# Sums of weight blocks by adding transfers from DRAM to DRAM, for both MLP products of a decoder layer

## The chip, the core and the metric

The kernel runs on one core of a Trainium2 chip. The metric is the device time of one execution in microseconds (us). One execution was also recorded by the hardware profiler; all lines marked as profile come from that one. PE is TensorE (matmuls), DVE VectorE, ACT ScalarE, POOL GpSimd, SP the engine that issues most of the transfers. Each engine works through its own queue of instructions strictly in order.

## The reference

One decoder layer over 1024 positions of 1024 features, in float32. What matters here is its last part:

```python
for i in range(DEPTH):
    h = rms_norm(x, norm_mix[i])
    p = h @ w_in[i]
    ...                                   # RWKV-7 heads and a short convolution, gated and merged
    x = x + merged @ w_out_mix[i]
    mem_n = rms_norm(mem, norm_mem[i])
    x = x + memory_cross_attention(rms_norm(x, norm_xattn[i]), mem_n, w_q[i], w_kv[i], w_xo[i])
    hm = rms_norm(x, norm_mlp[i])
    x = x + jnp.square(jax.nn.relu(hm @ w_up[i])) @ w_down[i]
return rms_norm(x, norm_final)
```

`w_up` is 1024 x 4096 and `w_down` 4096 x 1024, 16 MB each.

## The kernel before

Activations are kept transposed, features on partitions and positions along the free side, in two blocks of 512 positions (b = 0, 1). Every float32 operand is split into a high and a low part (ACT rounds the high part, DVE subtracts to get the low part), and each product is three matmuls: high x high, high x low, low x high. Weights come as tiles of [128, 8, 128] (512 KB): a load into a raw buffer (`wr`, two of them; `wr+`, `wh+`, `wl+` and `P` are taken from the large pool `H`), then the split into `wh` and `wl`. `wlist` is the list of all weight tiles in the order of use, `w_loads` issues their loads on SP, `w_splits` the splits.

There is no fixed schedule: the program is written as many small streams, and a planner (`Scheduler`) that estimates every instruction's time runs whichever stream is ready and so writes each engine's order once, when the kernel is built. `need(t)` is the planner's time at which `t` is written, `done` holds the keys of steps that were issued, and `until(...)` waits for such keys. On the chip, only semaphores order the engines.

Both MLP products are done as two-by-two blocks with seven block products in place of eight (numbers 1, 2, 6, 5, 7, 3, 4). That needs sums of blocks of both operands. The products are the same count before and after the change: 16 steps of 7 products in `up_products`, and 7 products of 4 column tiles in `mlp_down`. The sums of the activations are made on DVE and POOL (`up_operands`, `sums`). For the weights, with blocks a11, a12, a21, a22, the before makes

- for `w_up`, inside the product: a "quad" of two raw tiles is loaded, POOL makes four sums in them (`w_split_quad`), and ACT and DVE split the pieces;
- for `w_down`, ahead of it: `w_sums` starts when the mixer's merge is done. In 16 rounds, SP loads four blocks, POOL makes four sums of 128 x 512, and SP stores them to `d_s`, from which the down product loads them as weight tiles.

The order of the kernel is: projections and RWKV (to about 735 us), keys and values of the 256 memory tokens (`mem_k`, `mem_v`, weights `w_kv`), merge (`w_proj_b`, `w_proj_a`), `w_out_mix`, queries and attention (`w_q`), its output product (`w_xo`, which adds the residual loaded from `d_x`), the up product, the down product, final norm. `norm_side` makes the reciprocal root mean square of a block of positions: a matmul with `ones` sums the squares (`pss<-ones,ex`), POOL takes the power.

Nearly every instruction has line L253, the planner's call, so rows are told apart by their tiles.

Of the kernel before, what the change touches and what calls it, by code (L numbers as in the profile page):

```python
# [9 lines left out]
F32 = mybir.dt.float32  # L10
F32R = mybir.dt.float32r
# [6 lines left out]
P = 128  # L18
# [240 lines left out]
def tile_hybrid_block(  # L259
# [116 lines left out]
    wlist, light, quads = [], set(), set()  # L376
# [11 lines left out]
    def w_quad(w, c0):  # L388

        return [(w[:, c0 + t * P:c0 + (t + 1) * P].rearrange("(k p) n -> p k n", p=P), 0, KD) for t in range(2)], \  # L390
            [P, KD, P]

    def w_block(half, t, j, kh):

        c0 = (2 * j + half) * P
        return w_down[0, kh * 2048:(kh + 1) * 2048, c0:c0 + P].rearrange("(k t p) n -> t p k n", t=2, p=P)[t]


    ws = {"raw": 0, "split": 0, "made": 0, "closed": 0, "next": 0, "live": 0, "raws": {}, "tiles": {}, "sums": 0}
    w_key = {}  # L400

    def w_raw(i):
        n = 2 if i in quads else 1
        more = i >= first_quad and (i - first_quad) % 2 if i in quads else i > first_quad and i % 4 > 1
        raw = ws["raws"][i] = [sb("wr+" if more else "wr", wlist[i][1]) for _ in range(n)]
        ws["live"] += n
        return raw

    def w_load(i, raw):
        for n, (src, k0, k1) in enumerate(wlist[i][0]):  # L410
            SP.dma_start(raw[n if i in quads else 0][:, k0:k1, :], src)
        ws["raw"] += 1

    def w_loads():
        for i in range(2, len(wlist)):
            if i < first_quad:
                yield lambda: i < ws["split"] + 2
            else:
                yield lambda: ws["live"] + (2 if i in quads else 1) + ws["sums"] <= BUFS["wr"] + 2
            if i in w_key:  # L420
                yield until(*w_key[i])
            raw = w_raw(i)
            yield need(*raw) - 0.3
            w_load(i, raw)

    def w_sums():

        yield until("merged")
        ws["sums"] = 2
        for j in range(4):  # L430
            for kq in range(4):
                kh, k0 = kq // 2, 4 * (kq % 2)
                t, keys = {}, []
                yield lambda: ("h2", 0, 5) not in done or ("h2r", 1) in done
                for pair in (((0, 0), (1, 0)), ((1, 1), (0, 1))):
                    raw = sb("wr+", [P, 2, 4, P])
                    for n, m in enumerate(pair):
                        yield need(raw)
                        t[m] = raw[:, n]
                        SP.dma_start(t[m], w_block(*m, j, kh)[:, k0:k0 + 4, :])  # L440
                a11, a21, a22, a12 = (t[m] for m in ((0, 0), (1, 0), (1, 1), (0, 1)))
                for n, (dst, x_, y_, op) in {7: (a11, a11, a21, ALU.subtract), 5: (a21, a21, a22, ALU.add),
                                             6: (a22, a22, a11, ALU.subtract), 3: (a12, a12, a22, ALU.subtract)}.items():
                    yield max(need(x_, y_), pace("POOL", 0.6))
                    POOL.tensor_tensor(dst, x_, y_, op=op)
                    keys.append(("s", n, j, kq))
                    dma(d_s[n][j, kh][:, k0 * P:(k0 + 4) * P], dst.rearrange("p k n -> p (k n)"), keys[-1])
                yield until(*keys)
        ws["sums"] = 0
# [5 lines left out]
    def w_split_quad(raws):  # L455


        n = KD // 2
        ra, rb = (t[:].rearrange("p (k t) n -> p t k n", t=2) for t in raws)

        def tiles():
            more = "+" if ws["made"] % 3 == 2 else ""
            return sb("wh" + more, [P, 2, n, P], F32R), sb("wl" + more, [P, 2, n, P], F32R)

        def halves(hi, lo, src):
            ACT.activation(hi, src, AF.Copy)
            yield need(hi) - 0.3
            DVE.tensor_tensor(lo, src, hi.bitcast(F32), op=ALU.subtract)

        room_ = lambda: ws["made"] < ws["closed"] + 3  # L470
        yield room_
        hi, lo = tiles()
        yield from halves(hi[:], lo[:], ra)
        w_made(hi, lo)
        yield need(lo)
        s2 = sb("st", [P, n, P])
        POOL.tensor_tensor(ra[:, 0], ra[:, 0], rb[:, 0], op=ALU.subtract)
        POOL.tensor_tensor(s2[:], rb[:, 1], ra[:, 0], op=ALU.subtract)
        POOL.tensor_tensor(rb[:, 0], rb[:, 0], rb[:, 1], op=ALU.add)
        POOL.tensor_tensor(ra[:, 1], ra[:, 1], s2[:], op=ALU.subtract)  # L480
        yield room_
        hi, lo = tiles()
        yield need(s2) - 0.3
        yield from halves(hi[:, 0], lo[:, 0], s2[:])
        yield need(rb) - 0.3
        yield from halves(hi[:, 1], lo[:, 1], rb[:, 0])
        w_made(hi, lo)
        yield room_
        hi, lo = tiles()
        yield need(ra) - 0.3  # L490
# [1602 lines left out]
```

## Time and profile before

| what | value |
|---|---|
| median of 3 runs | 1842.07 us (1840.36 to 1845.47) |
| profiled execution, its own time | 1842.19 us |
| its span, first to last instruction | 1840.5 us |
| mean granted TensorE clock | 0.977 |
| DMA | 289.19 MB, 157 GB/s mean |
| TENSOR_TENSOR `P<-P,P` on DVE | 204 of 770 ns |

Busy time is the time in which an engine works on an instruction; a matmul's includes its pipeline, so two that follow each other overlap. "idle before" and the words in brackets tell what ended the wait of an engine. In the chain of waits each piece is what the next one waited for, followed back from the end of the program. In rows by stretches the columns are PE, weight loads, DVE, ACT and POOL, then the granted clock, the busy share of the 16 DMA engines and what they moved. `SPq` rows are transfers that SP issues; their length is SP's time, not the transfer's.

### The profile page before, as it was taken

The page shows a single profiled execution, that of the slowest core. Times are in us where ns is not written, and L with a number is a line of the kernel's source. Part 1 is how long each engine was busy: PE and PEld are TensorE (multiplying, and loading weights), DVE is VectorE, ACT ScalarE, POOL GpSimd, SP SyncE. Part 2 cuts the span into 40 slices and gives each one's busy share as a digit, 9 for nine tenths or more (in the row PEclk, how much of TensorE's full clock was granted, in tenths as well). Part 3 has the DMA queues.
Part 4 walks back from the last instruction along what each step waited for, and adds up shares of the span by engine and source line. Part 5 has one row for each costly group of instructions (what it writes and reads, how often), then busy time and mean ns, then how long its engine had stood idle before and what let it go on. Part 6 is the DMA issues. An engine that isn't in the chain of part 4 may idle for free.

```text
span 1840.5 us, 26663 instructions
## 1 busy us (share of the span) xinstructions
PE 1773.6 (96%) x9914; PEld 1434.2 (78%) x9914; DVE 1078.3 (59%) x1689; ACT 698.8 (38%) x1229; POOL 514.6 (28%) x867
## 2 busy tenths in 40 slices
PE   7999999999989999999999999989999999999998
PEld 6577776767768778988888877868888888888887
DVE  4377665666564432456556765586777775655543
ACT  6423333123234332422233333354444444543442
POOL 2016653755536110000223445242323220000000
PEclk9699998999999999999999999999999999999999
DMA  6443532333325444754655667415454469765431
GB/s 211 168 125 104 157 112 61 104 82 104 105 66 169 119 126 126 228 167 149 229 180 166 206 192 263 126 60 190 145 183 144 163 203 336 266 211 198 165 113 60
DMA packets 302751, 289.19 MB, mean 157 GB/s; under 512 B 40648, under 2 KB 223038, under 8 KB 302622
## 3 DMA queue, kind: packets, MB, share of 16 engines
q1 hardware_dynamic: 302606, 287.49, 48.8%
q8 instruction: 78, 1.28, 0.3%
q14 instruction: 51, 0.42, 0.1%
q10 hardware_dynamic: 16, 0.00, 0.0%
HBM read 193.06 MB, written 94.37 MB: 156 GB/s over the span
## 4 chain that ended last, share of the span: by engine, by line
PE 67%; DVE 5%; DMA 3%; issue 2%; ACT 2%; POOL 1%; SPq 0%; POOLq 0%; DVEq 0%; ACTq 0%
PE psg L253 44%; PE pss L253 11%; PE psc L253 8%; PE psy L253 3%; DVE P L253 3%; DMA wr<-in_w_kv_dram 2%; ACT P L253 1%; DVE wl L253 1%; POOL ex L253 1%; ACT wh L253 0%; DMA P<-d_v 0%; DVE st L253 0%; DVE sh L253 0%; DVE sm L253 0%; DMA P<-d_x 0%
## 5 line engine op out<-in xcount | busy, mean ns | idle before, releaser
L253 PE MATMUL psg<-H,wh 128*128 128x512 f32 (+1 forms) x1872 | 614.3, 406 | 4.3 <-DVE P L253 3.7
L253 PEld LDWEIGHTS psg<-H,wh 128*128 128x128 f32 (+1 forms) x1872 | 353.5, 192 | 84.3 <-issue 4.0
L253 PE MATMUL psg<-P,wh 128*128 128x512 f32 (+1 forms) x1240 | 370.7, 380 | 3.3 <-ACT wh L253 1.8
L253 PE MATMUL psg<-H,wl 128*128 128x512 f32 x920 | 372.3, 405 | 0.4 <-DVE wl L253 0.4
L253 PEld LDWEIGHTS psg<-P,wh 128*128 128x128 f32 x1240 | 228.3, 189 | 47.2 <-ACT wh L253 2.4
L253 PE MATMUL psg<-P,wl 128*128 128x512 f32 (+1 forms) x620 | 235.4, 380 | 0.0
L253 ACT ACTIVATE wh<-wr 128x1024 fp32r<-128x1024 f32 (+2 forms) x189 | 139.5, 767 | 245.3 <-PE psg L253 134.1
L253 DVE TENSOR_TENSOR wl<-wr,wh 128x1024 fp32r<-128x1024 f32 (+2 forms) x180 | 166.0, 945 | 90.7 <-ACT wh L253 90.1
L253 PEld LDWEIGHTS psg<-H,wl 128*128 128x128 f32 x920 | 177.1, 193 | 37.6 <-DVE wl L253 1.0
L253 ACT ACTIVATE P<-P 128x512 fp32r<-128x512 f32 (+3 forms) x242 | 147.0, 641 | 73.2 <-DVE P L253 39.9
L253 DVE TENSOR_TENSOR P<-P,P 128x512 fp32r<-128x512 f32 (+2 forms) x204 | 149.6, 770 | 16.4 <-ACT P L253 15.0
L253 POOL TENSOR_TENSOR sm<-sm,mhalf 128x8 f32<-128x8 f32 (+2 forms) x18 | 23.8, 1327 | 440.9 <-DVE sm L253 440.9
L253 PEld LDWEIGHTS psg<-P,wl 128*128 128x128 f32 x620 | 116.8, 188 | 21.7 <-DVE wl L253 0.5
L253 POOL TENSOR_TENSOR ex<-ex,P 128x60 f32<-128x60 f32 (+24 forms) x248 | 94.1, 379 | 50.3 <-DMA P<-dn 34.0
L253 POOL TENSOR_TENSOR ex<-ex 128x60 f32<-128x60 f32 (+24 forms) x248 | 97.9, 395 | 19.4
L253 PE MATMUL pss<-P,wh 128*128 128x512 f32 x296 | 91.7, 390 | 1.2 <-DVE P L253 1.2
L253 DVE TENSOR_SCALAR P<-psc,sm 64x64 f32<-64x64 f32 x120 | 34.9, 291 | 85.2 <-ACT P L253 80.6
L253 PE MATMUL psc<-P,P 128*64 128x64 f32 (+4 forms) x816 | 75.0, 257 | 9.8 <-DVE P L253 4.9
L253 ACT ACTIVATE P<-psc,sm 64x64 f32<-64x64 f32 (+1 forms) x128 | 42.5, 333 | 105.5 <-PE psc L253 64.2
L253 PEld LDWEIGHTS psc<-P,P 128*64 128x64 f32 (+4 forms) x816 | 48.1, 147 | 44.1 <-issue 20.8
L253 DVE TENSOR_TENSOR P<-psg,P 128x512 f32<-128x512 f32 x44 | 30.3, 689 | 86.6 <-PE psg L253 69.4
L253 PE MATMUL psc<-P,wh 128*128 128x512 f32 x216 | 66.9, 390 | 0.0
(671 smaller groups left out, 2754.7 us busy)
## 6 DMA issues: line engine op xcount, KB each, us to landing
P<-d_t SPq DMA_DIRECT2D x56, 512.0 KB
wr<-in_w_in_dram SPq DMA_DIRECT2D x42, 512.0 KB
d_t<-P SPq DMA_DIRECT2D x64, 256.0 KB
d_x<-P SPq DMA_DIRECT2D x48, 256.0 KB
P<-d_x SPq DMA_DIRECT2D x24, 512.0 KB
d_t<-st SPq DMA_DIRECT2D x48, 256.0 KB
d_tg<-st SPq DMA_DIRECT2D x32, 256.0 KB
wr<-in_w_kv_dram SPq DMA_DIRECT2D x16, 512.0 KB
```

Source lines behind the costliest of these rows:

```text
L253: return fn(*args, **kw)
```

## The change

The sums of weight blocks are made from DRAM to DRAM, for both products. For each sum SP copies one block (`put`), and POOL's queue then issues a transfer that adds another block to the destination as it writes (`add`, `accum_op=ALU.add`). Since a transfer only adds, the seven products are rewritten with other signs: the second half of the output columns comes out negated (the operand of product 6 is split with its sign turned, relu takes the minimum instead of the maximum there and the square hides it, the down product's second half is subtracted). The column tiles that belong together are now half a weight apart (m = j + 4 * half) instead of neighbours.

```diff
-    def w_sums():
-        yield until("merged")
-        ws["sums"] = 2
-        ...                     # 16 rounds: four loads, four POOL tensor_tensor, four stores
-    def w_split_quad(raws):
-        ...                     # four POOL tensor_tensor for each quad of w_up, splits of the pieces
+    def w_half(w, t, half):
+        n = w.shape[1] // 2
+        rows = w.rearrange("(k t p) n -> t k p n", t=2, p=P) if w.shape[0] == D else \
+            w.rearrange("(t k p) n -> t k p n", t=2, p=P)
+        return rows[t][:, :, half * n:(half + 1) * n]
+    def w_sums():
+        yield until(("win", len(ORDER) - 1))
+        def put(dst, src):
+            yield from quiet()
+            yield need(dst, src)
+            SP.dma_start(dst, src)
+        def add(dst, src):
+            yield need(dst) + 1.0
+            POOL.dma_start(dst, src, accum_op=ALU.add)
+        for w, sums, key, n in ((w_up[0], d_su, "su", 1), (w_down[0], d_s, "s", 2)):
+            a11, a21, a12, a22 = (w_half(w, t, half) for t in range(2) for half in range(2))
+            for q in range(w.shape[0] // (2 * n * P)):
+                ks = slice(q * n, (q + 1) * n)
+                s5, s7, s6, s3 = (sums[p][ks] for p in (5, 7, 6, 3))
+                for dst, first, then in ((s5, a21, a22), (s7, a11, a21), (s6, s5, a11), (s3, s6, a12)):
+                    yield from put(dst, first if first in (s5, s6) else first[ks])
+                    yield from add(dst, then[ks])
+                yield need(s3)
+                done.add((key, q))
...
-    wlist += [w_quad(w_up[0], 2 * P * i) for i in range(NP_)]
+    d_su = {p: scratch([KD // 2, P, DFF // 2], f"d_su{p}") for p in (5, 7, 6, 3)}
+    for i in range(NP_):
+        cs = slice(i * P, (i + 1) * P)
+        for m, pair in enumerate((((0, 0), (1, 0)), (6, 5), (7, 3), ((1, 1),))):
+            srcs = [d_su[q] if q in d_su else w_half(w_up[0], *q) for q in pair]
+            if m in (1, 2):
+                w_key[len(wlist)] = [("su", q) for q in range(4)]
+            wlist.append(...)   # one tile: two loads of 256 KB (one for the last)
...
-        yield need(acc[b])
+        yield need(acc[b]) + (6.0 if key == "h3r" else 0.0)      # norm_side
...
-            DVE.scalar_tensor_tensor(dst, src, 0.0, r[b][:], op0=ALU.max, op1=ALU.mult)
+            DVE.scalar_tensor_tensor(dst, src, 0.0, r[b][:], op0=ALU.min if half else ALU.max, op1=ALU.mult)
...
-    nc = _bacc.Bacc("TRN2", target_bir_lowering=False, num_devices=1, dynamic_dma_scratch_size=256)
+    nc = _bacc.Bacc("TRN2", target_bir_lowering=False, num_devices=1, dynamic_dma_scratch_size=1024)
```

A round of `w_up` is 4 copies and 4 adding transfers of 1 MB (4 rounds), one of `w_down` the same of 512 KB (8 rounds). In each round two of the copies (`s6` from `s5`, `s3` from `s6`) read what an adding transfer has written, so SP waits for that transfer.

SP's queue in the keys and values of the memory. Before, loads of `w_kv` alternate with stores of the keys:

```order
L253 DMA wr_7010<-in_w_kv_dram 128x8x128
L253 DMA d_kt<-st_7016 128x256
L253 DMA wr_7056<-in_w_kv_dram 128x8x128
L253 DMA d_kt<-st_7050 128x256
L253 DMA wr_7086<-in_w_kv_dram 128x8x128
L253 DMA d_kt<-st_7096 128x256
L253 DMA wr_7130<-in_w_kv_dram 128x4x256
```

Now, at the same place (`d_su_84` and `d_su_85` are the sums 5 and 7 of `w_up`, 128x2048 is 1 MB):

```order
L253 DMA wr_7034<-in_w_kv_dram 128x8x128
L253 DMA d_kt<-st_7040 128x256
L253 DMA d_su_84<-in_w_up_dram 128x2048
L253 DMA d_kt<-st_7069 128x256
L253 DMA wr_7082<-in_w_kv_dram 128x8x128
L253 DMA wr_7108<-in_w_kv_dram 128x8x128
L253 DMA P_7128<-d_tg 128x1024
L253 DMA d_kt<-st_7121 128x256
L253 DMA wr_7164<-in_w_kv_dram 128x4x256
L253 DMA d_kt<-st_7159 128x256
L253 DMA wr_7191<-in_w_kv_dram 128x4x256
L253 DMA d_kt<-st_7204 128x256
```

The first copy of the fourth round now stands between the second and third of these loads, and the second (`d_su_85`) follows the rows shown.

SP's queue at the end of attention. Before, the residual's loads (`P<-d_x`) stand between the stores and loads of the w_down sums:

```order
L253 DMA wr+_1387_10123<-in_w_down_dram 128x4x128 x2
L253 DMA wr+_1395_10150<-in_w_down_dram 128x4x128 x2
L253 DMA d_s_87<-wr+_1387_10123 128x512
L253 DMA d_s_85<-wr+_1387_10123 128x512
L253 DMA P_10222<-d_x_133 128x1024
L253 DMA P_10224<-d_x_133 128x1024
L253 DMA d_s_86<-wr+_1395_10150 128x512
```

Now the last copy between sums, `d_s_91<-d_s_90`, stands here:

```order
L253 DMA d_s_91<-d_s_90 16x8192
L253 DMA st_9516<-d_vm 128x2x256
L253 DMA wr_9545<-in_w_xo_dram 128x8x128
L253 DMA wr_9709<-in_w_xo_dram 128x8x128
L253 DMA st_9767<-d_kt 128x2x256
L253 DMA st_9843<-d_vm 128x2x256
L253 DMA wr_9871<-in_w_xo_dram 128x8x128
L253 DMA wr_10031<-in_w_xo_dram 128x8x128
L253 DMA P_10129<-d_x_137 128x1024
L253 DMA P_10131<-d_x_137 128x1024
```

The sums have moved ahead of the loads of `w_xo`, and nothing of them is left around the residual's loads.

PE's queue at the end of `w_xo`'s product (`psg<-H`) and the start of the up product (`psg<-P`). Before, the sum of squares of the first block stands inside the former:

```order
L253 MATMUL psg_10854<-H_9952,wl_10724 128x512
L253 MATMUL pss_10879<-ones_128,ex_10247 128x1 x4
L253 MATMUL psg_10854<-H_10277,wh_10723 128x512
L253 MATMUL psg_10854<-H_10278,wh_10723 128x512
L253 MATMUL psg_10854<-H_10277,wl_10724 128x512
```

Now it comes within the second of the up product's sums:

```order
L253 MATMUL psc_10800<-P_10420,wl_10620 128x512
L253 MATMUL psc_10800<-P_10691,wh_10619 128x512 x2
L253 MATMUL pss_10812<-ones_132,ex_10149 128x1 x4
L253 MATMUL psc_10800<-P_10691,wl_10620 128x512
L253 MATMUL psc_10800<-P_10766,wh_10619 128x512 x2
```

It has moved behind the last matmuls with `H` and behind seven of the up product's eight first groups.

More of the change, by code (lines that the diff above doesn't have):

```diff
@@ L422, in w_loads @@
             raw = w_raw(i)
-            yield need(*raw) - 0.3
+            yield need(raw) - 0.3
             w_load(i, raw)
     def w_sums():
-        yield until("merged")
-        ws["sums"] = 2
[L430 to L449, printed above, removed]
+        yield until(("win", len(ORDER) - 1))
[16 more added lines that the diff above has]
+                done.add((key, q))
     def w_made(hi, lo):
@@ L453, in w_made @@
         ws["made"] += 1
-    def w_split_quad(raws):
[L458 to L490, printed above, removed]
-        yield from halves(hi[:], lo[:], ra)
-        w_made(hi, lo)
-        yield room_
-        hi, lo = tiles()
-        yield from halves(hi[:, 0], lo[:, 0], rb[:, 1])
-        w_made(hi, lo)
     def w_splits():
@@ L519, in w_splits @@
                 continue
-            more = "+" if i > first_quad and ws["made"] % 3 == 2 else ""
+            more = "+" if i > first_mlp and ws["made"] % 3 == 2 else ""
             hi = sb("wh" + more, wlist[i][1], F32R)
```

88 lines of the change are left out of this document (42 added, 46 removed).

## The prediction

> **What bounds the kernel now.** I read the page first (busy shares, slices, chain), then the busy time of each engine by stage, then the chain of waits and the timelines of single engines at the few places where TensorE stands still.
>
> ```profile
> PE 1773.6 (96%) x9914; PEld 1434.2 (78%) x9914; DVE 1078.3 (59%) x1689; ACT 698.8 (38%) x1229; POOL 514.6 (28%) x867
> ...
> PE 67%; DVE 5%; DMA 3%; issue 2%; ACT 2%; POOL 1%; SPq 0%; POOLq 0%; DVEq 0%; ACTq 0%
> ```
>
> TensorE is busy for 96% of the span and makes 67% of the chain that ended last. So a change that leaves the matmuls alone (it does: the same seven products of the same size in both MLP halves) can only win where TensorE waits, and lose where it makes TensorE wait. The stages, from the busy times in stretches (columns: stretch, its length, busy us and instructions of PE, weight loads, DVE, ACT, POOL, granted clock, share of the DMA engines, GB/s):
>
> ```profile
> 640.00:735.00 95.00, 94.71 (x569) 75.88 (x566) 29.88 (x54) 29.19 (x56) 8.42 (x6) 1.00 0.41 125
> 735.00:785.00 50.00, 48.05 (x378) 46.01 (x378) 22.30 (x63) 25.51 (x77) 0.00 (x0) 1.00 0.74 221
> 785.00:1060.00 275.00, 274.11 (x1291) 227.93 (x1290) 165.65 (x259) 84.12 (x146) 61.36 (x42) 1.00 0.56 182
> 1060.00:1130.00 70.00, 62.38 (x317) 51.21 (x316) 41.87 (x88) 26.95 (x59) 29.70 (x21) 1.00 0.69 221
> 1130.00:1190.00 60.00, 60.00 (x267) 49.67 (x266) 31.56 (x33) 20.82 (x32) 18.63 (x12) 1.00 0.54 174
> 1190.00:1240.00 50.00, 40.81 (x174) 32.19 (x173) 38.84 (x48) 27.21 (x46) 25.45 (x18) 0.93 0.17 57
> 1240.00:1500.00 260.00, 260.00 (x1148) 215.28 (x1147) 186.88 (x225) 110.00 (x170) 79.89 (x56) 1.00 0.49 164
> 1500.00:1550.00 50.00, 50.00 (x222) 41.41 (x221) 32.87 (x46) 22.63 (x36) 1.39 (x1) 1.00 0.89 303
> 1550.00:1800.00 250.00, 250.00 (x1125) 207.41 (x1124) 135.90 (x174) 116.38 (x165) 1.02 (x1) 1.00 0.59 200
> ```
>
> Inside the MLP (1240 to 1800) TensorE has no gap at all, though POOL works 79.9 us there on the sums that the change takes away. So the obvious saving, POOL's and the splits' time in the MLP, is worth nothing. What is to be had lies ahead of it: 70 - 62.38 = 7.6 us at the end of attention (1060 to 1130) and 50 - 40.81 = 9.2 us where the up product begins (1190 to 1240). What is at risk is 735 to 785, the keys and values of the memory, where the DMA engines are busiest ahead of the MLP, 0.74.
>
> **The change, part by part.**
>
> *Sums of w_down on chip (POOL, SP, 16 rounds) go.* At the end of attention they hold up the kernel; the chain of waits shows how:
>
> ```profile
> 1088.26 3.94 DMA wr+_1368_9998<-in_w_down_dram
> ...
> 1100.13 4.94 DMA wr+_1387_10123<-in_w_down_dram
> ...
> 1106.57 1.31 POOL wr+_1387_10123 L253
> ...
> 1108.33 5.04 DMA P<-d_x
> ...
> 1113.46 0.69 DVE P L253
> ```
>
> SP is in order. Its loads of the residual, P<-d_x, stand behind stores of sums, those behind POOL, POOL behind loads of blocks. The residual lands at 1113.4, DVE waits for it with its first residual add, and the softmax steps of the last head queue behind that on DVE. Of the 7.6 us nearly all lies between 1090 and 1122. In the changed order no sum stands near: the last copy is four weight loads of w_xo ahead of P<-d_x. I take 6.5 back and leave 1.1, since P<-d_x is still released only by the attention output just ahead and costs its 5 us.
>
> *The quads of w_up go; each weight tile now is loaded alone.* At the start of the up product (rows of the timelines of SP, ACT, PE and DVE: start, length, engine, operation, count, in brackets the idle time ahead and what ended it):
>
> ```profile
> 1170.05 11.30 SPq L253 DMA_DIRECT2D wr<-in_w_up_dram  x2
> ...
> 1187.73 1.06 ACT L253 ACTIVATE wh<-wr 128x1024 fp32r<-128x1024 f32 x1 [8.16 <-issue]
> ...
> 1203.22 1.87 PE L253 MATMUL pss<-ones,ex 128*128 128x1 f32 x8 [5.84 <-DVE ex L253]
> ...
> 1206.38 1.05 PE L253 MATMUL psg<-H,wh 128*128 128x512 f32 x2
> ...
> 1209.61 0.62 PE L253 MATMUL psg<-P,wh 128*128 128x512 f32 x2
> ...
> 1216.78 5.99 DVE L253 TENSOR_TENSOR P<-P,P 128x512 fp32r<-128x512 f32 x8
> ...
> 1225.44 7.67 DVE L253 TENSOR_TENSOR P<-P,P 128x512 fp32r<-128x512 f32 x6
> ```
>
> The first quad needs two buffers; SP waits 11.3 us until the second is free, ACT's split of the quad then holds ACT idle for 8.2 us, the evacuations of the residual queue behind it, and the mean square (pss<-ones,ex) holds TensorE for 5.84 us, after which it runs slower for a while (two matmuls 1.05 against 0.62, at a granted clock of 0.93 over the stretch). In the change the first tile needs one buffer, free at 1170, so ACT isn't held; and the mean square stands 19 rows further down TensorE's queue (the 6 us added in norm_side). DVE's splits take 1.28 each beside POOL's quad sums (7.67 / 6) against 0.75 (5.99 / 8); POOL no longer sums there. There are 9.2 us of gaps and about 1.9 for the slow matmuls after the gap (nine, each (1.05 - 0.62) / 2 = 0.21 longer), 11.1 in all. What is late next is DVE, which has the same splits to make; I leave it 2.3 and take 8.8.
>
> *The sums move ahead, DRAM to DRAM, from the gating loads to the first load of w_xo:* 48 copies on SP (16 of 1 MB, 32 of 0.5 MB) and 48 adding transfers on POOL's queue. For neither is there a row in the trace. A copy: at least its bytes at the best rate that a stretch shows.
>
> ```profile
> 1130.00:1140.00 10.00, 10.00 (x46) 8.28 (x45) 4.09 (x5) 2.52 (x5) 2.59 (x2) 1.00 1.03 352
> ```
>
> ```profile
> 443.60 7.07 DMA P<-d_v
> ...
> P<-d_v SPq DMA_DIRECT2D x8, 256.0 KB
> ```
>
> At 352 GB/s 1 MB (1.05 million bytes) is 3.0 us of all 16 engines. The slowest large transfer on the chain is 256 KB in 7.07 us, 28 us per MB. An adding transfer lies between: not below a copy (3.0), since it moves at least the same bytes (a gain from it is excluded, nothing on a compute engine gets shorter by it), and at most 28. It reads two operands for one result, so I put it near the lower end, at 4.1, midway between a copy and POOL's own adds (1.31 us for 128 x 512, 256 KB, above; 5.2 per MB).
>
> Where this costs: before 735 the shares are 0.41 and weight tiles are loaded long ahead, so nothing. In the keys and values the loads are the chain:
>
> ```profile
> 738.70 6.75 DMA wr<-in_w_kv_dram
> ...
> 760.11 3.88 DMA wr<-in_w_kv_dram
> ...
> 764.55 1.44 DVE wl L253 x4
> ```
>
> Two buffers, a load of 4 to 7 us, a split of 2, the next load: any delay of a load is a delay of TensorE. SP's new order puts three copies of 1 MB between these loads, and three adds (the last of the third round, two of the fourth) run there: 3 x 3.0 + 3 x 4.1 = 21.3 us of all engines. Free are 50 x (1 - 0.74) = 13.0. The rest, 8.3 us, is lost. From 785 on a round is half as large, a weight tile of 48 matmuls lasts some 10 us (275 / 1291 x 48), and 16 rounds of POOL sums no longer load the engines: nothing.
>
> *The wait on SP and POOL.* Two of four copies in a round wait on SP for the add ahead of them; behind them stand weight loads. In SP's timeline the first copy of all follows the first of these rows, and the tightest round, the third of w_up, lies between the other two:
>
> ```profile
> 613.57 0.39 SPq L253 DMA_DIRECT2D sh<-d_g  x1
> ...
> 703.13 0.38 SPq L253 DMA_DIRECT2D wr<-in_w_kv_dram  x1
> ...
> 730.10 0.89 SPq L253 DMA_DIRECT2D P<-d_tg  x2
> ```
>
> That is 27 us for two copies (4 us each with SP's issue and landing, as the 3.88 us load) and two adds, one after the other. So an add may take 9.5 us from issue to landing before SP is late; the loads behind have some 5 us more. By my 4.1 plus 2 to 4 us of landing it fits. Behind POOL's waiting adds stand the gating products and the two small powers of the second norm; they are late by one copy, 4 us, and TensorE needs them a tile later: nothing.
>
> *Edits at nothing:* seven loads of 256 KB instead of two of 512 KB per pair of tiles (12 MB more in the up product, 40 GB/s on top of 164, hidden under matmuls; bare if the share, 0.49, reached 1); negated splits and relu (the same instructions, one of them scalar_tensor_tensor); sums read back in 512-byte pieces; column tiles paired otherwise.
>
> Sum, from the profiled execution's 1842.2 (span 1840.5 and 1.7 around it; the median of three is 1842.1): - 6.5 - 8.8 + 8.3 = 1835.2, so 1835.
>
> **The rivals.**
>
> *Adds at half a copy's rate: no change.* An add reads both operands from memory, so it holds the engines for twice a copy, 6.0 us per MB. Then 3 x 3.0 + 3 x 6.0 - 13.0 = 14.0 is lost in the keys and values and the time is 1840.9. For it: the 0.74 leaves no room. Against it: nothing measured here. The Trainium skill, "Collectives: The Full Stack", section "The bandwidth ceiling: the fold count and why AG ≠ RS ≠ AR", says this of a reducing transfer: the add itself is free, but two source reads go through the same read ring, so it moves half as fast as a copy. No run here shows it yet; by that rule the sum is this rival's 1841, and I give it a quarter.
>
> *Slow adds hold SP: slower.* If an add of 1 MB takes over 9.5 + 5 = 14.5 us to land, SP stands at each dependent copy, weight loads behind it miss their tile, and all four rounds of w_up lie on TensorE's path. At 20 us a round takes 2 x 4 + 2 x 20 = 48 us; four take 192, against 785 - 614 = 171 from the first copy to the end of the keys and values: 21 late, plus 8.3, less the two gains (15.3): 1856. At the far end, 28, a round takes 64, 256 in all, 85 late: 1920. For it: no adding transfer is in the trace, POOL issues them itself. Against it: 512 KB loads land in 4 to 7 us beside others.
>
> *The gains don't come: the stalls stay.* If DVE, not SP and ACT, sets the pace at 1090 to 1122 and 1190 to 1240 (38.84 of 50 us busy there), the sums' removal only moves the wait: 1842.2 + 8.3 = 1850, or 1843 with one of the two gains. Against it: ACT's 8.16 us and the late P<-d_x stand in the rows.
>
> **How the numbers follow.** A measurement of this kernel tells some 0.3%, 5.5 us, from no change. Forecast (two gains, adds near a copy): 0.46, ending between 1824 (both gaps gone, little lost) and 1837. Half rate: 0.24, 1837 to 1847. Slow adds: 0.18, 1848 to 1920. No gains: 0.12, of which 0.03 within 0.3%. So faster 0.46, same 0.27, slower 0.27. The range leaves out the top half of the slow adds and a little below: 1824 to 1862; the forecast's own is 1824 to 1838.
>
> **What would show it.** The stretch 1060 to 1130 with under 2 us of gaps and P<-d_x issued as soon as attention ends; no 8 us hole on ACT ahead of the up product; the keys and values longer by some 8 us, with DMA at 1.0; no wait of SP on an adding transfer above 5 us; the MLP without a gap and as long as before. The prediction is wrong if adds take over 10 us per MB, if SP's queue reaches the merge late, or if DVE refills the two holes.

## The result and the profile after

The change made the kernel slower: 1915.18 us median (1913.43 to 1917.47, four runs) against 1841.21 (1839.29 to 1845.47), a ratio of 1.0394, 95% interval 1.0366 to 1.0422. The profiled execution's span is 1913.7 us where it was 1840.5, so it shows 73.2 us of the loss. A few runs took over 6% longer than the others of their kernel (one of hybrid's twelve, two of before's thirteen beside fill, fill2 and beforenorm) and are in no ratio and no median below. First the rows of the page that answer to those of before: busy shares, the clock and DMA by slice, the DMA queues (packets, MB, share of 16 engines' span), and the adding transfers on POOL's queue (count, KB each, median us from issue to landing).

```profile
PE 1788.5 (93%) x9914; PEld 1447.5 (76%) x9914; DVE 1018.4 (53%) x1673; ACT 694.1 (36%) x1213; POOL 369.2 (19%) x787
...
PEclk9699999999989998899996989999999999999999
DMA  5543533313335999998987752435666659866531
...
q1 hardware_dynamic: 320398, 300.07, 48.9%
q0 software_dynamic: 11008, 33.56, 10.1%
...
PE 32%; issue 1%; DVE 0%; ACT 0%; POOLq 0%; POOL 0%; DVEq 0%; ACTq 0%
...
d_su<-in_w_up_dram POOLq DMA_DIRECT2D x16, 1024.0 KB, 11.5
d_s<-in_w_down_dram POOLq DMA_DIRECT2D x32, 512.0 KB, 7.4
```

The chain of waits (PE 32%) breaks off behind an adding transfer and doesn't help here. TensorE has the same 9914 matmuls, POOL 145 us less work, and still the span is longer. The DMA row shows the place: from 620 us on (slice 13, counted from 0) eight slices stand at 8 or 9 tenths, where before had 4 to 7:

```profile
DMA  6443532333325444754655667415454469765431
```

The queue rows give the price of a transfer: queue q0 carries only the adds, 33.56 MB, which is 32 times 1 MB (16 of 1 MB, 32 of half). 10.1% of 1913.7 us is 193.3 us of all engines: 6.04 us per MB. The rest, on q1, costs 0.489 x 1913.7 us for 300.07 million bytes: 3.27 us for each 1.0486 million, that is for 1 MB. This is the mean of all that q1 carries, not of the copies alone.

The stretches, cut so that each holds the work of a stretch shown of before (the columns are the same). The old 785 to 1060 is split in three, 828 to 1149:

```profile
742.00:828.00 86.00, 56.88 (x381) 53.90 (x380) 23.52 (x65) 27.46 (x82) 4.06 (x5) 0.83 0.98 287
828.00:995.00 167.00, 167.00 (x735) 138.20 (x734) 85.67 (x117) 40.98 (x57) 14.21 (x16) 0.99 0.85 229
995.00:1050.00 55.00, 24.67 (x101) 19.64 (x100) 10.68 (x17) 8.82 (x14) 8.51 (x9) 0.69 0.80 196
1050.00:1149.00 99.00, 90.57 (x456) 76.10 (x455) 51.55 (x121) 33.73 (x75) 9.09 (x10) 0.95 0.65 145
1149.00:1214.00 65.00, 62.03 (x317) 51.40 (x316) 38.59 (x91) 27.10 (x59) 0.65 (x1) 1.00 0.28 97
1274.00:1313.00 39.00, 37.01 (x173) 29.85 (x172) 32.27 (x45) 26.43 (x44) 10.89 (x8) 1.00 0.48 147
1313.00:1573.00 260.00, 260.00 (x1149) 215.29 (x1148) 157.72 (x213) 106.99 (x156) 0.00 (x0) 1.00 0.64 206
```

The keys and values (x381, before x378 in 50 us) take 86 us at a DMA share of 0.98. Between 995 and 1050 TensorE works 24.67 of 55 us. The end of attention (x317, before x317 in 70 us) takes 65, the start of the up product (x173, before x174 in 50) takes 39, and the up product has no gap, as before.

To put a number on every place I use that both kernels make the same number of matmuls: the time by which a given number of them is done says how late an execution is there. Of before and of the change:

```profile
0.00:940.00 940.00, 897.06 (x5852) 706.79 (x5853) 521.75 (x919) 320.83 (x619) 320.45 (x732) 0.96 0.45 138
```

```profile
0.00:983.00 983.00, 907.88 (x5852) 716.07 (x5853) 516.11 (x917) 318.26 (x616) 321.53 (x746) 0.94 0.60 172
```

After 5852 matmuls the change is 43 us late. Read so every 20 us of before (from rows like these, interpolated between stretches whose ends lie 2 us apart), the lateness grows by:

| from (us of before) | what runs there | the change |
|---|---|---|
| 600 to 720 | end of RWKV, gating | +6.7 |
| 720 to 800 | keys and values | +36.3 |
| 800 to 940 | merge, w_out_mix | +0.1 |
| 940 to 980 | second norm, first queries | +35.0 |
| 980 to 1040 | queries | -1.9 |
| 1040 to 1060 | attention begins | +12.6 |
| 1060 to 1140 | attention ends | -5.1 |
| 1140 to 1240 | w_xo, start of the up product | -10.7 |
| 1240 to 1800 | both MLP products | 0.0 |

So both gains came, 15.8 us in all, and were lost nearly six times over in four places. TensorE's longest gaps in the last three of them (timeline of TensorE: start, length, operation, in brackets the idle time ahead and what ended it):

```profile
766.47 0.80 PE L253 MATMUL psg<-P,wh 128*128 128x256 f32 x2 [14.43 <-ACT wh L253]
...
1003.81 1.66 PE L253 MATMUL pss<-ones,ex 128*128 128x1 f32 x8 [4.15 <-DVE ex L253]
...
1034.83 1.11 PE L253 MATMUL pss<-ident,sm 128*128 128x128 f32 x4 [24.88 <-POOL sm L253]
...
1122.43 0.69 PE L253 MATMUL psc<-ident,sh 128*128 128x128 f32 x2 [4.50 <-DVE sh L253]
...
1136.86 2.73 PE L253 MATMUL psy<-P,P 128*128 128x512 f32 x6 [3.93 <-DVE H L253]
```

The first is a weight tile of w_kv that ACT cannot split yet (it waited 16.18 us for the load). The second is the sum of squares of the second norm, behind DVE, which stood behind ACT: ACT had waited 6.84 us for a tile of w_q. The third is POOL's power for that norm. The last two come behind the tiles of keys and values that attention reads (ACT waited 5.44 us for `st<-d_kt` and 10.24 for `st<-d_vm`). Before, TensorE waited for nothing at the second norm (its row has no bracket):

```profile
959.74 0.60 PE L253 MATMUL pss<-ident,sm 128*128 128x128 f32 x4
```

What POOL, SP and DVE did in the change, from their timelines:

```profile
1011.33 0.88 POOL L253 DMA_DIRECT2D d_s<-in_w_down_dram  x1 [5.18 <-issue]
1021.13 0.90 POOL L253 DMA_DIRECT2D d_s<-in_w_down_dram  x1 [8.92 <-issue]
1032.82 0.89 POOL L253 DMA_DIRECT2D d_s<-in_w_down_dram  x1 [10.79 <-DMA d_s<-d_s]
1033.40 1.37 POOL L253 TENSOR_TENSOR sm<-sm,mhalf 128x4 f32<-128x4 f32 x1
```

```profile
989.51 0.48 SPq L253 DMA_DIRECT2D d_s<-d_s  x1
990.10 1.06 SPq L253 DMA_DIRECT2D wr<-in_w_q_dram  x1
...
1129.72 0.47 SPq L253 DMA_DIRECT2D d_s<-d_s  x1
1130.25 0.57 SPq L253 DMA_DIRECT2D st<-d_vm  x1
```

```profile
1005.51 0.16 DVE L253 TENSOR_SCALAR sm<-pss 128x4 f32<-128x4 f32 x1 [1.85 <-PE pss L253]
```

DVE had the sums of squares at 1005.7; POOL's power came at 1033.4, behind three adds that each waited. SP sent off the tile of w_q only at 990.10, after the copy ahead of it had waited since 976 for an add, and the load of a tile of values (st<-d_vm) only at 1130.25, after the copy ahead of it had waited since 1116. So the 35.0 us of the second norm are three things: 26.2 us of waits for POOL's powers (24.88 and, for the second block, 1.30), 4.15 us behind SP's late tile, and the remaining 4.7 us in slower matmuls around these gaps (two of 512 columns took 1.05 us there against 0.62, at a granted clock of 0.85, 0.50 and 0.90 in 990 to 1010, 1010 to 1035 and 1035 to 1050).

### The profile page after: what moved, and what is told of

Its sections match the earlier page's. It is cut to its first block, busy times and chain, and to the rows that moved or that the text cites. A ratio compares the mean times of both kernels' runs of the same rounds, so it can differ in the third digit from the quotient of the medians.

```text
span 1913.7 us, 26492 instructions
## 1 busy us (share of the span) xinstructions
PE 1788.5 (93%) x9914; PEld 1447.5 (76%) x9914; DVE 1018.4 (53%) x1673; ACT 694.1 (36%) x1213; POOL 369.2 (19%) x787
## 3 DMA queue, kind: packets, MB, share of 16 engines
q1 hardware_dynamic: 320398, 300.07, 48.9%
q0 software_dynamic: 11008, 33.56, 10.1%
HBM read 255.98 MB, written 144.70 MB: 209 GB/s over the span
## 5 line engine op out<-in xcount | busy, mean ns | idle before, releaser
L253 PE MATMUL psg<-P,wh 128*128 128x512 f32 (+1 forms) x1240 | 378.4, 387 | 21.8 <-ACT wh L253 20.7
L253 PEld LDWEIGHTS psg<-P,wh 128*128 128x128 f32 x1240 | 234.1, 194 | 66.5 <-ACT wh L253 21.6
L253 ACT ACTIVATE wh<-wr 128x1024 fp32r<-128x1024 f32 (+1 forms) x189 | 144.3, 792 | 291.0 <-PE psg L253 149.9
L253 PE MATMUL psg<-P,wl 128*128 128x512 f32 (+1 forms) x620 | 239.8, 387 | 0.0
L253 DVE TENSOR_TENSOR wl<-wr,wh 128x1024 fp32r<-128x1024 f32 (+1 forms) x180 | 165.5, 942 | 112.7 <-ACT wh L253 112.1
L253 POOL TENSOR_TENSOR sm<-sm,mhalf 128x8 f32<-128x8 f32 (+2 forms) x18 | 26.2, 1476 | 661.2 <-DVE sm L253 661.2
L253 DVE TENSOR_TENSOR P<-P,P 128x512 fp32r<-128x512 f32 (+2 forms) x184 | 127.8, 726 | 17.5 <-ACT P L253 16.2
L253 POOL DMA_DIRECT2D d_s<-in_w_down_dram x32 | 28.8, 901 | 273.5 <-issue 165.1
## 6 DMA issues: line engine op xcount, KB each, us to landing
d_su<-in_w_up_dram POOLq DMA_DIRECT2D x16, 1024.0 KB, 11.5
```

Source lines behind the costliest of these rows:

```text
L253: return fn(*args, **kw)
```

## The experiments

Three explanations were on the table. Bandwidth: the DMA engines are full, and the loads that TensorE needs are slow whoever waits. SP's queue: a copy that waits for an add holds the loads behind it. POOL's queue: an add that waits holds POOL's own instructions behind it. Each kernel below ran beside runs of before on the same chip. How late each profiled execution fell in the stages above (worked out in the same way; the first row is what it had before the sums begin):

| from (us of before) | change | nodep | ring | plain | powfirst | room | gate | early | fill | hybrid |
|---|---|---|---|---|---|---|---|---|---|---|
| 0 to 600 | 0.0 | -14.0 | -5.6 | -3.6 | -1.1 | -0.4 | 1.6 | 17.0 | 0.7 | -7.6 |
| 600 to 720 | 6.7 | 4.7 | 7.1 | 2.9 | 9.1 | 1.1 | 2.6 | 10.1 | 9.6 | 1.1 |
| 720 to 800 | 36.3 | 34.4 | 34.7 | 18.0 | 36.7 | 15.3 | 0.2 | 2.0 | 0.0 | 0.2 |
| 940 to 980 | 35.0 | 21.3 | 1.6 | 4.4 | 7.3 | 0.0 | -0.1 | -0.2 | -0.2 | 0.4 |
| 1040 to 1060 | 12.6 | 0.0 | 0.0 | 0.0 | 7.9 | 0.0 | 0.0 | 0.0 | 0.0 | 4.9 |
| 1060 to 1140 | -5.1 | -5.1 | -5.1 | -5.1 | 1.4 | -4.9 | -5.1 | -5.1 | 10.4 | 4.0 |
| 1140 to 1240 | -10.7 | -10.7 | -6.0 | -10.6 | -10.7 | 5.3 | -4.3 | -10.7 | -4.8 | -10.7 |
| 1240 to 1800 | 0.0 | 0.1 | 0.9 | 0.2 | 0.0 | 11.8 | 26.2 | 0.2 | 6.6 | 1.1 |

The first row is not an effect of an edit except in early, whose sums start at 195 us, and perhaps fill, whose sums start at 554; in the others they start after 600 (for nodep and hybrid see the last section). Each column is one execution, and it can differ from the median of its kernel: nodep's and hybrid's are the fastest of theirs, early's the slowest.

**nodep: no copy waits for an add.**

```diff
-        def put(dst, src):
+        def put(dst, src, seen):
...
-            yield need(dst, src)
+            yield need(dst, seen)
...
-                    yield from put(dst, first if first in (s5, s6) else first[ks])
+                    seen = first if first in (s5, s6) else first[ks]
+                    yield from put(dst, a11[ks] if first in (s5, s6) else seen, seen)
```

> The third and fourth copy of each round read a block of the weight in place of the sum before them, so SP waits for no adding transfer; bytes, number and order of the transfers stay (two of the four sums come out otherwise). Queue theory (adds land late, 11.5 us per MB, and what stands behind a waiting copy or a waiting add in SP's and POOL's queue is late with them): the keys and values go back from 85 to 50-56 us, the 24.9 us hole of TensorE before pss<-ident,sm shrinks below 8, time 1828 to 1850. Bandwidth theory (the DMA engines are full, share 0.9 to 1.0, and the weight loads are late whoever waits): the keys and values stay at 75 us or more, time 1885 to 1910.

Measured 1885.68 us (1871.46 to 1890.61), 1.022 of before (1.0174 to 1.0267). The place in attention, 12.6 us, is gone. That fits SP's queue, which the rows of SP above show; nodep by itself doesn't prove it, since its last add goes off at 1090.98, some 6 us into that stage. The keys and values lost 34.4 us all the same: there SP's waiting is not the cause, against my queue theory. The hole before pss<-ident,sm shrank only to 19.1, against under 8 expected, since POOL still stood; the waits of nodep name no transfer for it (engine, tile, what ended the wait, us in total, times, longest):

```profile
POOL d_s L253 <- issue: 196.1, 27, 10.5
```

The landings in the trace tell what it was. Nearly every one of these adds starts 0.31 us after the one before it has landed: one lands at 1001.85, the next starts at 1002.16. In the change it is the same (1011.01 and 1011.33), 165.1 us in all.

**ring: nodep with more memory for the descriptors of POOL's transfers** (and so with the same two sums made otherwise).

```diff
-    BUFS = {"H": 44, "wr": 2, ...
+    BUFS = {"H": 43, "wr": 2, ...
-    ... dynamic_dma_scratch_size=1024)
+    ... dynamic_dma_scratch_size=4096)
```

> As the kernel called nodep (no copy waits for an add), with four times the memory for the descriptors of POOL's transfers and one buffer less in the large pool. If POOL, having no room for a second add's descriptors, stands until the add before has gone (waits of 6 to 10 us called issue ahead of each add): these waits fall below 2 us, the power is made as soon as its sum of squares is there and the 19.1 us hole of TensorE ahead of pss<-ident,sm shrinks below 4; time 14 to 20 us below nodep's 1885. If POOL waits for something else: waits and hole stay within 4 us.

Measured 1873.73 us (1867.98 to 1879.47, two runs), 1.0156 of before (1.0103 to 1.0208): by the medians 12 us below nodep where 14 to 20 were expected, with intervals that overlap. The waits with no releaser fall from 196.1 to 1.6 us. POOL now waits for SP's copies, as written in the code; adds overlap (one starts at 995.69 while the one before it lands at 1000.30), and the power, behind the same 36 adds as in nodep, is made early enough (waits, then TensorE's timeline):

```profile
POOL d_s L253 <- DMA d_s<-in_w_down_dram: 215.5, 28, 20.9
```

```profile
997.68 0.65 PE L253 MATMUL pss<-ident,sm 128*128 128x128 f32 x4 [1.49 <-POOL sm L253]
```

The stage of the second norm loses 1.6 instead of 21.3 us. So POOL stood in two ways: for copies, by semaphore, and without one until the add before had landed. Since only the memory for descriptors (and one buffer of H) differs, room for descriptors is the likely reason for the second. The keys and values stay at +34.7. The start of the up product gains 6.0 in place of 10.7; whether the missing buffer is why was not tested.

**powfirst: no add while the second norm's powers are due.**

```diff
         def add(dst, src):
             yield need(dst) + 1.0
+            yield lambda: ("h2", 0, 5) not in done or ("h2r", 1) in done
             POOL.dma_start(dst, src, accum_op=ALU.add)
```

> POOL issues no adding transfer while the powers of the second norm (h2r) are outstanding; all else as in the change. If the 24.9 us hole comes from POOL's power standing behind three adding transfers: hole below 5 us, 24 to 35 us won, time 1880 to 1891. If the weight tiles of w_q, issued late by SP, would hold TensorE there anyway: under 12 us won, time above 1903.

Measured 1893.4 us (1891.26 to 1895.04), 1.0274 of before (1.0259 to 1.029): about 22 us won, a little under what I expected. The stage of the norm falls from 35.0 to 7.3, and TensorE's wait for POOL is no longer there; the wait for DVE's ex behind SP's late tile stays, 4.19 us. Part comes back in attention, whose end no longer shows the gain (+1.4 instead of -5.1), since the adds held up moved there. Together with ring this settles most of the 35 us: the power behind waiting adds.

**plain: each add a plain copy** (so no sums are made).

```diff
-            POOL.dma_start(dst, src, accum_op=ALU.add)
+            POOL.dma_start(dst, src)
```

> Each adding transfer on POOL's queue becomes a plain copy of the same block; same order and waits, no addition (the sums are not made). If the addition is what makes a transfer long (two reads for one write): engine time per MB falls from 6.0 to about 3.3 us, landing of 1 MB from 11.5 to 6-8 us, and the time to 1850-1880. If POOL's own queue is what is slow, or SP's waits come from elsewhere: landing stays above 10 us and the time within 10 us of 1915.

Measured 1844.84 us (1836.94 to 1854.43), 1.0006 of before (0.9987 to 1.0026), a little better than I expected. The queue, the bytes written and SP's order are the same:

```profile
q0 software_dynamic: 6912, 33.56, 5.6%
...
d_su<-in_w_up_dram POOLq DMA_DIRECT2D x16, 1024.0 KB, 7.8
d_s<-in_w_down_dram POOLq DMA_DIRECT2D x32, 512.0 KB, 4.8
```

5.6% of the 1845.0 us span over 32 MB is 3.23 us per MB, against 6.04 with the addition: 1.87 times. That is close to what the Trainium skill says of a reducing transfer ("Collectives: The Full Stack", section "The bandwidth ceiling: the fold count and why AG ≠ RS ≠ AR"): two reads for one write, half a copy's rate; here the rate agrees. The reason isn't shown: the page counts the same 255.98 MB read from memory with and without the addition, and the adds come in more packets (11008 against 6912). Landing falls from 11.5 to 7.8 us. Something else goes with the addition: POOL's waits without a releaser fall from 165.1 to 0.7 us, though the memory for descriptors is that of the change, and TensorE's wait for the power to 2.9. So both have a part in the second norm's fall from 35.0 to 4.4 us here. Without the addition the change would have been no change.

**room: the planner gives each add more time.**

```diff
         def add(dst, src):
-            yield need(dst) + 1.0
+            late = 6.0 if dst.shape[0] == 1 else 3.0
+            yield need(dst) + 1.0 + late / 2
             POOL.dma_start(dst, src, accum_op=ALU.add)
+            yield need(dst) + late
```

> Same work and same result, but the planner adds 6 us (1 MB) or 3 us (512 KB) to each adding transfer before it places the next copy, and half of that between a copy and its add; rounds spread to the end of the up product. Queue theory: SP and POOL hardly wait, only the two gains remain, time 1825 to 1840. Bandwidth theory: the six to eight transfers of 1 MB that still lie in the keys and values cost 15 to 25 us there, time 1845 to 1870.

Measured 1868.38 us (1866.07 to 1872.18), 1.0142 of before (1.0121 to 1.0163), as the bandwidth theory had it, though not all of it for its reason. The norm and attention lose nothing, and the keys and values 15.3 us with fewer transfers in them. New is the up product, +5.3 and +11.8, where the last rounds now lie: TensorE waits 11.7 us once, until 1221.66, for an operand whose sums POOL could make only from 1216.98 on, behind adds that had waited 18.47 and 7.68 us (POOL's queue again). The 11.8 are not traced further; the DMA share is 0.90 over the stretch:

```profile
1205.00:1425.00 220.00, 199.44 (x849) 162.55 (x849) 126.43 (x172) 89.65 (x137) 28.87 (x26) 0.94 0.90 253
```

**gate: room, and no copy in the keys and values or at the two norms.**

```diff
+        clear = lambda: not n0 < ws["raw"] < n0 + 17 and all(
+            (k, 0, 5) not in done or (k + "r", 1) in done for k in ("h2", "h3"))
         def put(dst, src):
+            yield clear
             yield from quiet()
```

> As the kernel called room, and no copy is placed while the w_kv tiles are loaded or the second or third norm is outstanding; rounds still begin where the change begins them and reach further into the up product. Bandwidth theory: keys and values back to 50-53 us (65 in room); the powers wait for nothing; but the sums that now lie in the up product meet its own loads (share 0.6 without them) and cost 8 to 20 us there: time 1838 to 1855. If the keys and values are long for another reason than the sums' transfers: over 60 us there.

Measured 1866.37 us (1854.78 to 1870.14), 1.0103 of before (1.0069 to 1.0137), above my range. The keys and values (first row), and the stretch in the up product (second):

```profile
739.00:790.00 51.00, 49.06 (x387) 47.28 (x386) 22.66 (x64) 25.73 (x78) 0.00 (x0) 1.00 0.73 223
```

```profile
1313.00:1573.00 260.00, 249.45 (x1083) 204.96 (x1082) 150.38 (x201) 101.59 (x149) 14.32 (x16) 0.98 0.95 280
```

With no sum in them the keys and values lose 0.2 us, at a share of 0.73, before's 0.74: the 36 us there are the sums' transfers. What was kept out of there is paid in the MLP, 26.2 us, where the share now is 0.95 and TensorE has gaps (17.9 us from 1233 to 1573, behind ACT, which waits up to 11.3 us for `P<-d_t`; full engines and SP's queue were not separated there). From 800 to 1140 gate has sums too, 10 adds of 1 MB and 6 of half, and loses nothing; nor does room with 7 and 14.

**early: the rounds begin at the first chunk of RWKV, otherwise as gate.**

```diff
-        yield until(("win", len(ORDER) - 1))
+        yield until(("win", 0))
```

> Same work and result. The rounds begin when the first of the eight chunks of RWKV has been inverted, not the last; each add has 6 us (1 MB) or 3 us (512 KB) more time until the next copy; no copy is placed while the w_kv tiles are loaded or the second or third norm is outstanding. If all losses come from where the sums lie (engines full in the keys and values, POOL's powers behind adds): only the two gains remain, time 1825 to 1836. If the sums cost wherever they are put (ahead of 735 the small loads of RWKV and POOL's own work there stand beside them): 1845 to 1865.

Measured 1846.03 us (1842.25 to 1853.74), 1.0014 of before (0.9992 to 1.0036): the same as before, at the lower end of my second case. From 720 on nothing but 2.0 us is lost and both gains stand, 15.8; but 17.0 us are lost up to 600, nearly all after the sums began at 195, and 10.1 more to 720. So RWKV, at a share of 0.68 from 200 to 640, is held up by the sums as well (before has a share of 0.37 there); by which of the three ways was not separated. The profiled execution is the slowest of ten, 7.7 us above the median, so a median one loses less ahead of 720. From 800 to 1140 it has 22 adds of half an MB and loses nothing.

**fill and fill2: two rounds of w_up ahead of the keys and values** (8 and 9 adds), **the rest closer together.**

```diff
-        yield until(("win", len(ORDER) - 1))
+        yield until(("win", 6))                    # fill2: ("win", 5)
...
+            late = (2.0 if ws["raw"] <= n0 else 0.0) * (2 if dst.shape[0] == 1 else 1)   # fill2: 3.0, 1.5
```

> Same work and result. Rounds start one chunk of RWKV earlier, two rounds of w_up end ahead of the keys and values; none is placed while the w_kv tiles are loaded or the second or third norm is outstanding; after the keys and values they follow each other as close as in the change, so that the last of w_down is placed at the first tile of the up product. Bandwidth theory: keys and values 50-53 us, no hole ahead of the powers, nothing lost in the up product; left are the tiles of keys and values of attention behind a blocked SP (up to 12 us, as in the change) and a few us ahead of 735: time 1828 to 1848. If the rounds fall behind their plan and reach into the up product: 1850 to 1865.

> As the kernel called fill, but rounds start two chunks earlier and each add has 3 us (1 MB) or 1.5 us (512 KB) more time until the next copy, so that three rounds of w_down lie in the up product. Less waiting of SP in attention (under 5 us lost there) against 4 to 5 us for each round in the up product: time 1836 to 1856.

Measured 1861.58 us (1857.98 to 1865.72), 1.0092 of before (1.0065 to 1.0119), and 1865.26 us (1857.37 to 1872.15), 1.0113 (1.0077 to 1.0149); fill ended where its second case lay, fill2 above its range. In both the keys and values are clean (0.0 and 1.6 us lost), and the loss moved: fill pays 9.6 ahead of 720, 10.4 at the end of attention, where TensorE waits 12.2 us once for DVE's sh, and 6.6 in the MLP; fill2 pays 20.0 up to 720 (its sums start at 499) and 18.2 in the MLP.

**norm0 and beforenorm: what the 6 us in norm_side do.** norm0 is the change without them, beforenorm the kernel before with them.

```diff
-        yield need(acc[b]) + (6.0 if key == "h3r" else 0.0)
+        yield need(acc[b]) + 0.0
```

> The change without the 6 us added in norm_side. If the quads' second buffer was what held the start of the up product (ACT's 8 us hole): the time stays within 4 us of 1915. If the later place of the mean square in TensorE's queue is what removed the gap: 5 to 9 us come back, 1920 to 1924.

> The kernel before with the 6 us added in norm_side and nothing else. If the later place of the mean square in TensorE's queue is by itself a part of the gain at the start of the up product: 3 to 6 us below before. If the quad's second buffer holds ACT, and so the mean square, wherever it stands: within 2 us of before.

Measured for norm0 1924.55 us (1918.76 to 1927.58), 1.0437 of before (1.0405 to 1.0468): by the two ratios 0.0043, or 8 us, above the change, with intervals that overlap. That is where my second case lay, but the profile shows less, 4.4 us at this place. For beforenorm 1843.18 us (1831.27 to 1849.56), 0.9991 (0.9969 to 1.0013): no difference. In the profiles the stage 1140 to 1240 gains 6.3 us in norm0 and 2.4 in beforenorm, against 10.7 with both edits. TensorE's wait for the mean square was 5.84 us before; in norm0 it is

```profile
1283.05 1.86 PE L253 MATMUL pss<-ones,ex 128*128 128x1 f32 x8 [2.87 <-DVE ex L253]
```

and in the change there is none. So by these single executions both edits count, the rest of the change (the quads' removal, as I take it) for more; beforenorm's 2.4 us doesn't show in its time. But ACT's hole, to which I had given the whole stall, stands in the change just as before (timeline of ACT):

```profile
1271.48 1.06 ACT L253 ACTIVATE wh<-wr 128x1024 fp32r<-128x1024 f32 x1 [8.16 <-issue]
```

**hybrid: only the w_up sums by adds, as in gate; w_down's on chip.** (Its w_down sums take the blocks a12 and a21 exchanged, so they are not the sums that the product needs, against the "same result" below; the number and size of instructions and transfers are those of the right sums.)

```diff
-        for w, sums, key, n in ((w_up[0], d_su, "su", 1), (w_down[0], d_s, "s", 2)):
+        for w, sums, key, n in ((w_up[0], d_su, "su", 1),):
...
+    def down_sums():                       # 16 rounds as in the kernel before
+        yield until("merged")
+        ...
+                for p, dst, y_ in ((7, a11, a21), (5, a21, a22), (6, a22, a11), (3, a12, a22)):
+                    POOL.tensor_tensor(dst, dst, y_, op=ALU.add)
+                    ...
```

> Same result. Only the w_up sums are made by adding transfers (placed as in the kernel called gate); the w_down sums are made on chip as before, POOL adding in two raw tiles of each round (all four sums as additions, to fit the new signs). Half the adding bytes and none in the up product or the keys and values: about 4 us lost ahead of 735 (as in gate), the start of the up product 8 to 11 us won, the end of attention as before or a few us worse where POOL's sums stand behind an add: time 1834 to 1842 where before takes 1843 to 1845. If adds and on-chip sums get in each other's way in POOL's and SP's queues: 1848 to 1865.

Measured 1843.76 us (median of eleven runs, 1835.8 to 1851.05), 1.0007 of before (0.9988 to 1.0026): the same, and above my first case by 2 us. The 10.7 us at the start of the up product are won whole, and nearly as much, 4.9 and 4.0, is lost in attention. The last adds (until 1042.87) and the on-chip sums lie side by side ahead of it, at a DMA share of 1.01 from 1000 to 1034; what exactly holds TensorE there was not separated. No version that was run beats the kernel before.

## Why the prediction was wrong

It said 1835 us, at most 1862; it is 1915. Two steps failed: what stands behind POOL's waiting adds was priced at nothing and cost most of 35.0 us, and the keys and values were priced at 8.3 us and cost 36.3. By its own steps:

- *End of attention, -6.5:* measured -5.1. *Start of the up product, -8.8:* measured -10.7. Sum 15.3 against 15.8. These sizes hold, the second partly by luck, for the reason given for it does not: "ACT isn't held" is refuted by the 8.16 us that still stand; the stall shrank from 5.84 to 2.87 us with the quads gone and vanished with the later place of the mean square. At the end of attention 3.0 us of gaps are left (65.00 - 62.03), where the prediction left 1.1. How the quads' work delayed the mean square was not separated further.
- *Keys and values, +8.3:* the mechanism was right, engines full at 1.0, and the term was mis-sized twice. An add costs 6.04 us of all engines per MB, not 4.1; the 6.0 of the rival "adds at half a copy's rate" was the right price. And not three copies and three adds fall into the stretch but five of each (POOL issues five between 742 and 828, SP a copy at 755, 771, 787, 803 and 824), since a stretch that is held up lasts long enough for the next round (the last copy mostly falls behind its end, but the one sent off at 738 still runs at its start). Counted so after the fact, the same sum gives 5 x 3.27 + 5 x 6.04 - 13.0 = 33.6; measured 36.3. For plain, with five of each too, it gives 5 x 3.27 + 5 x 3.23 - 13.0 = 19.5, measured 18.0; in gate there are no transfers to add, and 0.2 was measured.
- *"Behind POOL's waiting adds ... they are late by one copy, 4 us, and TensorE needs them a tile later: nothing":* this step failed worst. The power was 28 us late (1005.7 to 1033.4), behind three adds and not one, and TensorE had only 4 us of work left to cover it (its last matmul ahead of the hole ends at 1009.95): a hole of 24.88 us, and 35.0 with the late tile of w_q and the slower matmuls around. powfirst and ring, each in its own way, removed the hole. Ahead of 735, 6.7 us are lost, 4.8 of them from 600 to 640; a gating product stands there behind an add (the add waits 9.56 us until 635.67, the product behind it starts at 636.84), but that this is the cause was not tested.
- *"From 785 on ... nothing":* true of the weight tiles (0.1 us lost from 800 to 940 at a share of 0.85), false of the loads behind a waiting copy: a tile of w_q at the second norm, 4.15 us, and the small loads of keys and values for attention, 12.6 us, gone in nodep.
- *The wait on SP, late above 14.5 us for an add:* an add took 11.5 us to land, inside that bound, and SP's waiting still cost those two places. The bound counted two adds in one round, and not what stands behind a copy in attention. The mechanism of the rival "slow adds hold SP" was there, at another place than it named.
- *The MLP without a gap and as long as before:* right, also for the smaller loads (share 0.64, not 0.49). The rival that the gains stay away did not happen. *The chances:* the half rate and the held SP happened together with the gains, and an effect that was priced at nothing was as large as the largest. They were weighed one by one, as if only one could come.

The sum as measured: 6.7 + 36.3 + 0.1 + 35.0 - 1.9 + 12.6 - 5.1 - 10.7 = 73.0 of the 73.2 us.

## What to carry to other kernels

A sum made by transfers is not free work but work moved to the DMA engines: copy and add cost 3.27 + 6.04 us of all engines per MB here, 298 us for the 32 MB, and it costs nothing only where the engines and the queues have room. The sums cost time ahead of 600, in the keys and values, in the up product and, where they follow each other closely, at the second norm and in attention. Spread out from 800 to 1140, 11 to 14 MB of them cost nothing (room, gate, early), but no version found such a place for all 32. Before moving work to an in-order queue, list every small instruction that stands behind it there (a power of 1.4 us held TensorE for 24.9), and ask of each wait by how many of the slow steps it can be late, not by one. When a stretch is at its DMA limit, count the transfers that fall into the longer stretch, not into the old one.

## What the runs showed of the hardware that was not expected

POOL can stand ahead of a transfer that it issues without waiting for any semaphore: in nodep it waited 6 to 10 us ahead of most adds of w_down, 196.1 us in all, until 0.31 us after the one before it had landed, and no longer (1.6 us in all) when the memory for descriptors was four times as large. Plain copies of the same size, with the small memory, did not make it wait (0.7 us).

Executions can differ at their start by some 9 us without any edit there: of the profiled ones, nodep's and hybrid's were ahead after 120 us, by 9.0 and 8.0. Of before, and of hybrid, whose sums start only after 600:

```profile
60.00:80.00 20.00, 18.08 (x31) 8.56 (x30) 3.39 (x7) 6.75 (x10) 0.59 (x3) 0.50 0.47 179
```

```profile
60.00:80.00 20.00, 18.27 (x48) 9.41 (x48) 3.39 (x7) 8.83 (x14) 0.59 (x3) 0.80 0.56 213
```

The granted clock in these 20 us was 0.50 in the one and 0.80 in the other, and 31 against 48 matmuls were done. That explains the -7.6 of hybrid and 9.0 of the -14.0 of nodep in the table (the rest of nodep's comes between 350 and 600 and is not explained), and why single executions a few us apart tell nothing here unless the stages are compared.
